# One sum of squares instead of two in the column products of further norm groups

## The chip, the cores and the metric

The kernel runs on one core of one Trainium2 chip. The metric is the device time of one execution in microseconds (us). It ran three times before the change: 1835.74, 1836.15 and 1836.15 us, with a median of 1836.15. Five engines work side by side and are named as in the profile: PE (matrix products; PEld is its loading of weights, which overlaps PE), DVE (vector engine), ACT (scalar engine), POOL (GpSimd) and SP (which here issues transfers). Engines wait for one another by semaphores.

## The reference

A small decoder trunk in f32 with two layers works on 528 tokens of width 1024 (16 meta tokens and 512 tokens). Each layer has a SwiGLU feed-forward at half weight, a token mixer, and a second feed-forward at half weight. The mixer is gated linear attention (GLA) in layer 0 and sliding-window attention (SWA) in layer 1. The SWA uses one set of keys and values made once, after layer 0. Every sub-layer is normed on its input and on its output:

```python
def rmsnorm(x, g):
    y = x * lax.rsqrt(jnp.mean(x * x, axis=-1, keepdims=True) + EPS)
    return y * g

for layer in range(2):
    g = norm_gains[layer]
    h = h + 0.5 * rmsnorm(swiglu(rmsnorm(h, g[0]), w_ffn_in[layer, 0], w_ffn_out[layer, 0]), g[1])
    hn = rmsnorm(h, g[2])
    mix = gla_mixer(hn, ...) if layer == 0 else swa_mixer(hn, ..., k_shared, v_shared)
    h = h + rmsnorm(mix, g[3])
    h = h + 0.5 * rmsnorm(swiglu(rmsnorm(h, g[4]), w_ffn_in[layer, 1], w_ffn_out[layer, 1]), g[5])
    if layer == 0:
        k_shared, v_shared = split(rmsnorm(h, g_kv) @ w_kv)
```

The change concerns the sum over the 1024 features in `mean(x * x)` and nothing else.

## The kernel before, in words

Features lie on the 128 partitions and tokens along the free axis. A row of 1024 features is therefore 8 tiles (`KD` = 8, index k), and `H` is the residual stream and `Y` the output of a sub-layer in that layout. Tokens are worked in two groups: `L0 = [(0, 272), (272, 256)]` in layer 0 and `L1 = [(16, 256), (272, 256)]` in layer 1. They are called group 0 and group 1 here (gi in the code).

**Exact products.** To keep f32 accuracy each operand is split into a high and a low half. The operand `x_<name>` of a projection is built by `Operand.build`: ACT scales H by the gain and rounds it (L591, the high half), and DVE makes the low half (L227 is the line through which all of DVE's operations are recorded). A projection then takes three matmuls for each weight tile and k: two with the high half, one with the low half. Weights are streamed from HBM (`raw`) and split in the same way by ACT (L295, L317) and DVE (`w`, `w_s`).

**A norm.** The squares of the 8 tiles are summed over k into a tile `acc_<name>` by `square_into` (L559 and L561 square on ACT, L562 adds on POOL). With `parts` 1 the first square starts the sum and each of the other seven goes to a scratch tile and is added by POOL. With `parts` 2 the last square (k = 7) is not added: ACT writes it straight into a second sum. Then `root` sums over the partitions: for each column chunk of 128 tokens (of 68, in the group of 272 tokens) and for each of the sums it issues one f32 matmul with a column of ones, into `st_<name>`. The profile shows each such f32 product as two matmuls. A chain of small operations follows (`av`, `yv`, `zv`, `wv`), on DVE for the post-norms and on POOL for most operands, which ends in a diagonal `dg_<name>`. A matmul with ones spreads it over the partitions as `r_<name>` (called the factor). For a post-norm (`Residual.run`) DVE multiplies Y by r, adds the product to H, and the next operand is built from that H, k by k, and its squares are summed. For an operand, r is copied to `R_<name>` (L619) and applied by DVE after the projection (`gu<-x,R`), so that the projection can begin before r is known.

**Order.** PE's order is written by hand: the program is a set of generators, driven by a planner (`Flow`) with a clock of its own. Each matmul advances the clock by what it charges: n/2400 us for n columns of the split type, at least 0.12 for an f32 product. When the clock passes the time for which a job is due, its next step is placed, and a job's `yield d` says after how much of the clock it goes on. Jobs are looked at (`flow.pump`) after each of the low-half matmuls of a projection. In `x_first` these come as the last four of every twelve matmuls (four weight tiles times three, for one k), and group 0 has 96 matmuls there (8 k) before group 1 begins with its own 96. The other engines' order is made by a scheduler from the program's dependences.

The delays that matter here:

- `Residual.run` waits `1.8 + (ADDED if parts == 1 else 0)` before the products of a post-norm (L645), then `DCHAIN` = 3.0 plus `factors[gi]` before its factor r (L528).
- `Operand.factors` waits `FACT` = 1.5, plus `ADDED` where `parts` is 1, before its products, then `CHAIN` = 5 or `DCHAIN`, and more by name, before r.
- `ADDED` = 1.4; `CROWDED` = 1.8 is the `factors[1]` of the post-norm named l1f1, `SLACK` = 1.0 that of l1m.

**Names.** `into(name, ...)` makes a pair: the residual step (post-norm) at the end of one sub-layer and the operand of the next. l0m stands between layer 0's first feed-forward and GLA, l0f1 between GLA and the second feed-forward, kv between that and the shared keys, l1m between layer 1's first feed-forward and SWA, and l1f1 between SWA and the last feed-forward. The profile leaves the last digit out, so l0f1 appears as l0f and l1f1 as l1f. The last post-norm, "out", is made without `into`.

Of the kernel before, what the change touches and what calls it, by code (L numbers as in the profile page):

```python
# [28 lines left out]
L0 = [(0, 272), (272, 256)]  # L29
L1 = [(16, 256), (272, 256)]  # L30
# [41 lines left out]
V_KVN = 96  # L72
# [72 lines left out]
def trunk_kernel(ctx: ExitStack, tc, a, out, last_out):  # L145
# [12 lines left out]
    vec = cp.tile([P, V_N], F32, name="vec")  # L158
# [8 lines left out]
    def pair_tile(name, dt=F32R):  # L167
        return hp.tile([P, 2, TOK], dt, tag="pair", name=name)
# [5 lines left out]
    def flat(t):  # L174
        return t.rearrange("p a t -> p (a t)")
# [25 lines left out]
    def gain(layer, i, k):  # L201
        c = V_GAIN + layer * 48 + i * 8 + k
        return vec[:, c : c + 1]
# [427 lines left out]
    class Residual:  # L631
# [44 lines left out]
        def turn(self, g, sums):  # L676
# [10 lines left out]
            def turn_four(into, src, c, q):  # L687
                b = into[c][q] = ps(f"turn_{self.name}{c}{q}")
                for k in range(4):
                    transpose(b[:, k * P : (k + 1) * P], src[:, 4 * q + k, o + c * P : o + (c + 1) * P])  # L690
# [460 lines left out]
    class Gated(Item):  # L1151
# [8 lines left out]
        def into(self, hid):  # L1160
            self.hid = hid
            scratch = flat(pair_tile(f"c{self.name}", F32))
            n = self.n
            self.u2, self.g1, self.v = (scratch[:, i * n : (i + 1) * n] for i in range(3))
            self.h = scratch[:, n : 3 * n]
# [706 lines left out]
    sp.dma_start(ident, a["ident"])  # L1872
    dve.memset(eps, 1e-6)

    def into(name, layer, i, half, gv, groups, parts=(1, 2), post=(1, 2)):
        nxt = Operand(name, gv, groups, parts=parts)
        return nxt, Residual(name, layer, i, half, nxt, post)


    nxt, fin = into("l0m", 0, 1, True, lambda k: gain(0, 2, k), L0, (1, 1))  # L1880
    ffn(x, L0, fin, True)
    x = nxt
    nxt, fin = into("l0f1", 0, 3, False, lambda k: gain(0, 4, k), L0)
    gla(x, fin)
    x = nxt
    nxt, fin = into("kv", 0, 5, True, lambda k: vec[:, V_KVN + k : V_KVN + k + 1], L0, (1, 1))
    nxt.more = BUSY
    fin.factors[0] = SLACK_KV
    ffn(x, L0, fin, tail=8)
# [2 lines left out]
    with tc.tile_pool(name="kp", bufs=1) as kp:  # L1892
        x, own = Operand("l1f0", lambda k: gain(1, 0, k), L1), nxt

        def again(gi):
            while (1, KD - 1) not in own.ready:
                yield SCORE
            for k in range(KD):
                x.build(gi, k)
                yield 1.0  # L1900

        kv, placed = shared_kv(nxt, kp, [again(0), again(1)])
        x.rt, x.rjob, x.roots = nxt.rt, nxt.rjob, 0
        nxt, fin = into("l1m", 1, 1, True, lambda k: gain(1, 2, k), L1, (1, 1))
        fin.factors[1] = SLACK
        roots = kp.tile([P, 2, 4], F32, name="roots")
        nxt.column = [(roots[:, 0, 2 * g : 2 * g + 2], roots[:, 1, 2 * g : 2 * g + 2]) for g in range(2)]
        ffn(x, L1W, fin)
        x = nxt
        nxt, fin = into("l1f1", 1, 3, False, lambda k: gain(1, 4, k), L1, post=(2, 2))  # L1910
        fin.factors[1] = CROWDED
        flow.wait(placed)
        swa(x, kv, fin)
# [96 lines left out]
```

## Time and profile before

| what | value |
| --- | --- |
| median of the three runs | 1836.15 us |
| the profiled execution's own time | 1835.98 us |
| its span, first instruction to last | 1834.2 us |
| granted clock of PE over the span | 9 of 10 or more in all 40 slices |
| adds of squares on POOL for post-norms (L562) | 77, of 0.74 us in the median |

A row of a group reads: line, engine, operation, output <- inputs with their shapes, count, busy time, mean length in ns, then the idle time of the engine before it and what ended it. A row of the timeline reads: start, length, engine, line, operation, output <- inputs, count of like instructions that were joined into the row, and in brackets the idle time before it with its releaser. Matmuls overlap, so the length of a joined row runs past the start of the next, and the time that PE gives to a group is read from start to start. A row of the waits reads: the waiting engine and line, what it waited for, then the total, the number of waits and the longest. Of a kernel's stretch the windows give the engine's busy time.

### The profile page before, as it was taken

How to read it: one execution, taken by the hardware profiler on the slowest of the kernel's cores; microseconds unless marked ns; L12 is line 12 of the kernel's file. 1: busy time of each engine (PE TensorE's matmuls, PEld its weight loads, DVE VectorE, ACT ScalarE, POOL GpSimd, SP SyncE). 2: the span in 40 equal slices, each digit the busy share in tenths (PEclk: the TensorE clock that was granted, in tenths of full speed). 3: DMA queues.
4: the chain of work that ended last, by engine and by line, in shares of the span. 5: the costliest groups of instructions: out<-in, count | busy, mean ns of one | idle time of the engine just before them, and what ended most of it. 6: DMA issues, size and time to landing. Idle time of an engine off the chain costs nothing.

```text
span 1834.2 us, 38756 instructions
## 1 busy us (share of the span) xinstructions
PE 1825.8 (100%) x14696; PEld 1772.8 (97%) x14696; DVE 1481.2 (81%) x3029; ACT 1137.5 (62%) x2643; POOL 333.3 (18%) x499
## 2 busy tenths in 40 slices
PE   9999999999999999999999999999999999999998
PEld 9999999999999999999999899999988898999998
DVE  6889888679785788888878789888776678899884
ACT  6666665655576566665665566666666866666564
POOL 2210101330001411010133110202320142111122
PEclk9999999999999999999999999999999999999999
DMA  7755758433234366666853565759430226667681
GB/s 246 197 153 152 173 147 235 170 117 88 57 129 144 106 174 156 155 168 151 249 188 104 137 166 140 185 150 242 168 107 22 70 93 165 161 153 177 152 255 51
DMA packets 146251, 277.45 MB, mean 151 GB/s; under 512 B 16400, under 2 KB 36752, under 8 KB 146064
## 3 DMA queue, kind: packets, MB, share of 16 engines
q1 hardware_dynamic: 114208, 198.15, 33.9%
q0 software_dynamic: 31424, 76.23, 20.8%
q8 instruction: 115, 1.88, 0.4%
q10 hardware_dynamic: 432, 0.59, 0.1%
q14 instruction: 72, 0.59, 0.1%
HBM read 236.05 MB, written 38.34 MB: 150 GB/s over the span
## 4 chain that ended last, share of the span: by engine, by line
PE 92%; DVE 3%; ACT 2%; DMA 1%; issue 1%; SPq 0%; DVEq 0%; ACTq 0%
PE a L206 30%; PE x L206 18%; PE y L206 17%; PE c L206 14%; PE d L206 7%; ACT s L1729 1%; PE o L206 1%; PE po L206 1%; DVE w L227 1%; DMA raw<-in_w_in 1%; DMA H<-in_h 1%; DVE s L227 1%; DVE w_s L227 1%; DVE raw L227 1%; PE ps L206 0%
## 5 line engine op out<-in xcount | busy, mean ns | idle before, releaser
L227 DVE TENSOR_TENSOR w<-raw,w 128x512 fp32r<-128x512 f32 (+1 forms) x556 | 356.7, 666 | 28.8 <-ACT w L295 23.7
L227 DVE TENSOR_TENSOR w_s<-raw,w_s 128x512 fp32r<-128x512 f32 (+1 forms) x432 | 275.2, 647 | 78.3 <-ACT w_s L317 74.2
L317 ACT ACTIVATE w_s<-raw 128x512 fp32r<-128x512 f32 (+1 forms) x432 | 250.9, 593 | 94.4 <-DVE raw L227 90.8
L227 DVE TENSOR_TENSOR raw<-raw,raw 128x512 f32<-128x512 f32 (+1 forms) x312 | 194.9, 631 | 3.2
L376 POOL DMA_DIRECT2D raw<-in_w_in x112 | 105.6, 988 | 449.3 <-DVE w L227 169.0
L317 ACT ACTIVATE w<-raw 128x512 fp32r<-128x512 f32 (+1 forms) x324 | 185.0, 590 | 0.0
L295 ACT ACTIVATE w<-raw 128x512 fp32r<-128x512 f32 x232 | 133.8, 620 | 2.1 <-PE y L206 1.2
L206 PE MATMUL y<-hidl0f,w 128*128 128x272 f32 (+1 forms) x960 | 119.4, 285 | 0.0
L206 PEld LDWEIGHTS y<-hidl0f,w 128*128 128x128 f32 x960 | 118.0, 188 | 0.2
L206 PE MATMUL a<-zl0f_t,w_s 128*128 128x264 f32 x864 | 117.3, 285 | 0.0
L206 PE MATMUL y<-hidl1f,w 128*128 128x256 f32 (+1 forms) x768 | 114.9, 310 | 0.0
L206 PE MATMUL a<-zl1f_t,w_s 128*128 128x256 f32 x864 | 114.0, 281 | 0.0
L206 PEld LDWEIGHTS y<-hidl1f,w 128*128 128x128 f32 x768 | 105.0, 188 | 8.5
L1274 POOL DMA_DIRECT2D kept_y<-dn x32 | 36.8, 1149 | 405.6 <-DVE w_s L227 164.4
L206 PEld LDWEIGHTS a<-zl0f_t,w_s 128*128 128x128 f32 x864 | 110.3, 188 | 0.0
L562 POOL TENSOR_TENSOR acc_post<-acc_post,sq_post 128x256 f32<-128x256 f32 (+1 forms) x77 | 61.2, 796 | 264.4 <-ACT sq_post L561 260.9
L206 PEld LDWEIGHTS a<-zl1f_t,w_s 128*128 128x128 f32 x864 | 107.2, 188 | 0.0
L206 PE MATMUL x<-x_l0m,w 128*128 128x256 f32 (+1 forms) x768 | 102.2, 289 | 0.0
L206 PE MATMUL x<-x_l0f,w 128*128 128x256 f32 (+1 forms) x768 | 98.3, 287 | 1.6 <-ACT w L295 0.8
L206 PEld LDWEIGHTS x<-x_l0f,w 128*128 128x128 f32 x768 | 94.9, 189 | 3.0 <-DVE w L227 1.4
L206 PEld LDWEIGHTS x<-x_l0m,w 128*128 128x128 f32 x768 | 95.8, 188 | 1.6 <-issue 0.8
L206 PE MATMUL x<-x_l1f,w 128*128 128x256 f32 (+1 forms) x576 | 93.2, 321 | 0.0
(551 smaller groups left out, 4116.1 us busy)
## 6 DMA issues: line engine op xcount, KB each, us to landing
raw<-in_w_in SPq DMA_DIRECT2D x408, 256.0 KB, 4.3
raw<-in_w_in POOLq DMA_DIRECT2D x112, 256.0 KB, 5.4
raw<-in_w_down SPq DMA_DIRECT2D x128, 192.0 KB, 2.4
raw<-in_gla_in SPq DMA_DIRECT2D x52, 256.0 KB, 3.3
raw<-in_w_last SPq DMA_DIRECT2D x48, 256.0 KB, 5.2
kept_y<-dn POOLq DMA_DIRECT2D x16, 528.0 KB, 8.3
raw<-in_w_out SPq DMA_DIRECT2D x32, 256.0 KB, 3.4
kept_y<-dn POOLq DMA_DIRECT2D x16, 512.0 KB, 8.8
```

The lines of the kernel that those rows point to most:

```text
L206: inst = pe.matmul(o, lhs, rhs, start=start, stop=stop, skip_group_check=onto)
L227: made = op(*args, **named)
L295: high = act.activation(w[:, 0, :m], raw[:, :m], AF.Copy)
L317: act.activation(w[:, 0, :m], src, AF.Copy)
L376: added = pool.dma_start(r, src, accum_op=ALU.add)
L562: pool.tensor_tensor(sums[0][:, :n], sums[0][:, :n], t[:, :n], op=ALU.add)
L1274: pool.dma_start(y_sum[:, 2 * self.q : 2 * self.q + 2, o : o + 2 * n], self.y[:, :, : 2 * n], accum_op=ALU.add)
L1729: act.activation(s[:, c], s[:, c], AF.Exp, scale=rc[:, c % 2 : c % 2 + 1], bias=nm[:, c : c + 1], accum_out=den[:, c : c + 1],)
```

## The change

The defaults of `into` become one sum for both groups, in the operand (`parts`) and in the post-norm (`post`). The explicit `(1, 1)` of l0m and kv, which set the operand, become superfluous and are dropped; that of l1m stays. The explicit `post=(2, 2)` of l1f1 is dropped, so that it takes the default.

```diff
-    def into(name, layer, i, half, gv, groups, parts=(1, 2), post=(1, 2)):
+    def into(name, layer, i, half, gv, groups, parts=(1, 1), post=(1, 1)):
         nxt = Operand(name, gv, groups, parts=parts)
         return nxt, Residual(name, layer, i, half, nxt, post)
...
-    nxt, fin = into("l0m", 0, 1, True, lambda k: gain(0, 2, k), L0, (1, 1))
+    nxt, fin = into("l0m", 0, 1, True, lambda k: gain(0, 2, k), L0)
...
-    nxt, fin = into("kv", 0, 5, True, lambda k: vec[:, V_KVN + k : V_KVN + k + 1], L0, (1, 1))
+    nxt, fin = into("kv", 0, 5, True, lambda k: vec[:, V_KVN + k : V_KVN + k + 1], L0)
...
-        nxt, fin = into("l1f1", 1, 3, False, lambda k: gain(1, 4, k), L1, post=(2, 2))
+        nxt, fin = into("l1f1", 1, 3, False, lambda k: gain(1, 4, k), L1)
```

What each name has, as number of sums of (group 0, group 1):

| name | operand before | operand after | post-norm before | post-norm after |
| --- | --- | --- | --- | --- |
| l0m | (1, 1) | (1, 1) | (1, 2) | (1, 1) |
| l0f1 | (1, 2) | (1, 1) | (1, 2) | (1, 1) |
| kv | (1, 1) | (1, 1) | (1, 2) | (1, 1) |
| l1m | (1, 1) | (1, 1) | (1, 2) | (1, 1) |
| l1f1 | (1, 2) | (1, 1) | (2, 2) | (1, 1) |

The number changes in eight groups, six of post-norms and two of operands. The delays that depend on it (`ADDED`) change with it. The opening operand, with (2, 2), and "out", with (1, 2), are not touched.

## The prediction

> **What bounds the kernel now.** I read the page's first part and chain, then the waits of the matmul engine, then the timeline around the column products.
>
> ```profile
> span 1834.2 us, 38756 instructions
> PE 1825.8 (100%) x14696; PEld 1772.8 (97%) x14696; DVE 1481.2 (81%) x3029; ACT 1137.5 (62%) x2643; POOL 333.3 (18%) x499
> PE 92%; DVE 3%; ACT 2%; DMA 1%; issue 1%; SPq 0%; DVEq 0%; ACTq 0%
> ```
> ```profile
> PE busy L1821 <- DVE eps L227: 1.0, 1, 1.0
> PE x L206 <- ACT w L295: 0.8, 2, 0.4
> PE x L206 <- DVE w L227: 0.7, 2, 0.3
> ```
>
> PE is the kernel: 1825.8 of 1834.2 us busy, 92% of the chain, and the whole list of what it waited for (these are its largest entries) holds about 3 us. So the time is the sum of PE's instructions. Removing some saves their time one for one; any wait that is newly exposed on PE costs one for one. I therefore count two things: matmul pairs that go, and lost cover ahead of the instructions that PE reads next.
>
> **What goes.** A group of 256 tokens has two column chunks. The timeline of PE shows both kinds of group for the same norm (start, duration, operation, count):
>
> ```profile
> 1311.84 0.50 PE L206 MATMUL st_post_l1m<-ones,acc_post 128*128 128x1 f32 x4
> 1312.20 3.82 PE L206 MATMUL y<-hidl1f,w 128*128 128x256 f32 x30
> 1329.38 0.95 PE L206 MATMUL st_post_l1m<-ones,acc_post 128*128 128x1 f32 x8
> 1330.18 1.65 PE L206 MATMUL x<-x_l1m,w 128*128 128x256 f32 x12
> ```
>
> With one sum the products hold PE from 1311.84 to 1312.20, 0.36 us for 4 matmuls; with two from 1329.38 to 1330.18, 0.80 us for 8. The difference is 0.44 us a group. By the diff's arguments eight groups change: the second group of the post-norms l0m, l0f1, kv and l1m, both groups of post-norm l1f1, and the second group of operands l0f1 and l1f1. 8 x 0.44 = **-3.5 us**. It is all on PE, so all on the path.
>
> **What is added.** Eight adds on GpSimd, one per group:
>
> ```profile
> L562 POOL TENSOR_TENSOR acc_post<-acc_post,sq_post 128x256 f32<-128x256 f32 x56 | 42.7, 763 | 190.1 <-ACT sq_post L561 186.8 <-DVE H L227 3.2
> 366.78 0.40 ACT L559 ACTIVATE acc_post<-Y 128x256 f32<-128x256 f32 x1
> 369.39 0.95 PE L206 MATMUL st_post_l0m<-ones,acc_post 128*128 128x1 f32 x8
> ```
>
> That is 8 x 0.76 = 6.1 us on an engine that is 18% busy. In l0m the last square, which today goes straight into its own sum, ends at 367.18; the products start at 369.39. The add would end near 368.0 even in today's order, so PE would not wait for it. Two adds of the next norm stand on GpSimd's queue about there; they cost at most another 1.8 us, and the products themselves come later (next part). I cost the adds at nothing; without that cover one add is 0.76 us on the path.
>
> **What moves.** This is where the gain may go. A group with one sum waits ADDED = 1.4 more on the planner's clock before its products are put into PE's order (L645, L605). The clock charges 0.107 to a 256-token matmul and jobs are placed only at the last four of every twelve, so 1.4 becomes 12 matmuls. What those take in fact, and what follows from it at the tightest place, the second group of post-norm l1f1, is in these rows:
>
> ```profile
> 1484.17 0.95 PE L206 MATMUL st_post_l1f<-ones,acc_post 128*128 128x1 f32 x8
> 1484.97 4.46 PE L206 MATMUL x<-x_l1f,w 128*128 128x256 f32 x36
> 1489.28 0.50 PE L206 MATMUL st_l1f<-ones,acc_l1f 128*128 128x1 f32 x4
> 1487.74 0.42 DVE L227 TENSOR_TENSOR dg_post_l1f<-ident,yv_post_l1f 128x256 f32<-128x256 f32 x1
> L206 PE MATMUL x<-x_l1f,w x81: 274/280/365, 1480.3 to 1491.0; 128*128 128x256 f32 x81
> 1491.14 0.60 PE L206 MATMUL r_post_l1f<-dg_post_l1f,ones 128*128 128x256 f32 x2
> 1491.78 0.43 DVE L227 TENSOR_TENSOR r_post_l1f<-Y,r_post_l1f 128x256 f32<-128x256 f32 x1 [3.61 <-PE r_post_l1f L206]
> 1492.24 0.42 DVE L227 TENSOR_TENSOR H<-r_post_l1f,H 128x256 f32<-128x256 f32 x1
> 1492.70 0.51 ACT L591 ACTIVATE x_l1f<-H,vec 128x256 fp32r<-128x256 f32 x1 [2.62 <-DVE H L227]
> ```
>
> From 1484.97 to 1489.28 there are 36 matmuls in 4.31 us, 0.12 us each: 12 are **1.44 us**. The factor's product r_post starts after 81 of the 96 first-group matmuls; 15 are left, about 1.8 us and 0.25 for r_post itself. From r_post to the first build of the second group (multiply, add, scale) it is 1491.14 to 1493.21, 2.07 us. The two are equal: no slack today. The diagonal is ready at 1488.16, 3 us ahead, so the place of r_post is set by the planner, not by data. Twelve matmuls later only 3 are left, and PE has nothing else in its order: it stands about **+1.4 us**. The later builds shift with the first one, and PE with them, so this is paid once.
>
> The same shift of 1.44 us strikes the other second groups against the slack of their last build:
>
> ```profile
> 379.05 13.52 PE L206 MATMUL x<-x_l0m,w 128*128 128x272 f32 x111
> 388.61 0.96 DVE L227 SCALAR_TENSOR_TENSOR x_l0m<-H,vec,x_l0m 128x256 fp32r<-128x256 f32 x1
> 392.41 0.50 PE L206 MATMUL st_l0m<-ones,acc_l0m 128*128 128x1 f32 x4
> 617.93 7.82 PE L206 MATMUL x<-x_l0f,w 128*128 128x256 f32 x63
> 623.55 0.48 DVE L227 SCALAR_TENSOR_TENSOR x_l0f<-H,vec,x_l0f 128x256 fp32r<-128x256 f32 x1
> 625.58 0.95 PE L206 MATMUL st_l0f<-ones,acc_l0f 128*128 128x1 f32 x8
> ```
>
> - l0m: the 111 matmuls are 3 of the first group, 96 of the second and 12 of the next unit. The last build's low half is first read 16 matmuls before 392.41, at 390.5; it is ready at 389.57. Slack 0.9 us against 1.44: **+0.5 us**; bounds 0 (the scheduler may put the build ahead of a weight split) and 1.4.
> - l0f1: the low half is first read 4 matmuls before 625.58, at 625.1, and ready at 624.03. Slack 1.1: **+0.4 us**, bounds 0 and 1.4.
> - l1m: its r_post moves to where l1f1 has it today, where PE shows no wait: **+0.1 us**, bounds 0 and 1.4 (if its scale comes late).
> - kv has the sizes and places of l0m; its builds are not held behind weight splits at that point. I take 0 and let l0m's 0.5 bound it.
> - l1f1's first group: its products are among the attention's last output products and its builds are read some 5 us on; 0.
>
> **The operands.** For l1f1 and l0f1 the second operand factor is moved as well. Rows of l1f1, the last one from a window of 0.04 us around the first product that reads the last tile of h:
>
> ```profile
> 1507.91 0.95 PE L206 MATMUL st_l1f<-ones,acc_l1f 128*128 128x1 f32 x8
> 1515.75 0.59 PE L206 MATMUL r_l1f<-dg_l1f,ones 128*128 128x256 f32 x2
> 1516.38 0.38 ACT L619 ACTIVATE R_l1f<-r_l1f 128x256 f32<-128x256 f32 x1 [5.32 <-PE r_l1f L206]
> 1516.80 0.42 DVE L227 TENSOR_TENSOR gu<-x,R_l1f 128x256 f32<-128x256 f32 x1 [5.27 <-ACT R_l1f L619]
> 1516.80:1534.10 17.30, 17.20 (x32) 1.00 0.38 91
> 1533.37 0.69 DVE L227 TENSOR_TENSOR hidl1f<-gu,hidl1f 128x512 fp32r<-128x512 f32 x1
> 1534.89 0.63 PE L206 MATMUL y<-hidl1f,w 128*128 128x512 f32 x2
> ```
>
> DVE sits idle 5.27 us for R, then is busy 17.20 of 17.30 us, up to the last tile of h, ready at 1534.06. PE reads it with the second matmul of that row, near 1535.1: slack 1.05 us. Nothing in between gives time back. The shift of R is 1.4 to 2.8 us (one or two places of the planner, here with matmuls twice as wide); taken at 2.25, PE stands **+1.2 us**, bounds 0 and 1.8. For l0f1, with 272-token tiles and fewer products in between, I take **+0.2 us**, bounds 0 and 1.0.
>
> **Sum.** -3.5 + 1.4 + 0.5 + 0.4 + 0.1 + 1.2 + 0.2 = **+0.3 us**. The profiled execution took 1835.98 us, its span and 1.8 around it; the median shown is 1836.15, 0.17 above. From the median the change gives **1836.4 us**.
>
> One more thing the adds can do is hold DVE (start, duration):
>
> ```profile
> 1812.23 0.16 DVE L227 TENSOR_TENSOR zv_post_out<-zv_post_out,av_post_out 128x2 f32<-128x2 f32 x1
> 1812.32 0.73 POOL L562 TENSOR_TENSOR acc_post<-acc_post,sq_post 128x256 f32<-128x256 f32 x1 [3.44 <-ACT sq_post L561]
> 1812.43 0.64 DVE L227 SCALAR_TENSOR_TENSOR wv_post_out<-zv_post_out 128x2 f32<-128x2 f32 x1
> ```
>
> A DVE operation of 0.16 us takes 0.64 here, and ends as the add of GpSimd beside it ends. So an added add may cost DVE up to 0.5 us by this row, 8 x 0.5 = 4 us in all if each meets such an operation. DVE has 353 us idle and none of the eight adds falls into the stretch 1516.8 to 1534.1, where it has none, so I take 0; the upper bound for the place where it matters (l1f1's last builds) is one such meeting, 0.5 us.
>
> The Trainium skill, page "SBUF — State Buffer", section "Who interferes with whom", states the reason as a rule: a DVE instruction with two SBUF inputs and a GpSimd instruction that reads SBUF exclude each other, the later one being blocked for the whole of the earlier. The two rows agree with it, though the blocked operation has tiny inputs. By the rule all eight adds speak against the change; the sum would be +0.8 instead of +0.3 if one meets the path.
>
> **Rivals.**
> 1. *Everything but l1f1's first build is covered.* For it: a shift of 1.44 us against slacks of 0.9 to 1.1 leaves only small remainders, and the tile scheduler may order DVE anew. Then -3.5 + 1.4 = -2.1, **1834.1 us**; if the planner leaves r_post where it is too, -3.5, 1832.6.
> 2. *Slower: the late R of l1f1 backs up DVE.* DVE has no gap from 1516.8 on, so lateness there also holds weight splits, and with them the transfers that refill their buffers, and the next tiles PE needs. It decides from the point where all stalls pass 3.5 + 3.7 = 7.2 us, against the 3.8 of my sum; R's shift at its end of 2.8, paid twice (tile of h, then weights), and 1.4 in l0m and l0f1 each give 1.4 + 2.8 + 2.8 + 2.8 = 9.8, so -3.5 + 9.8 = +6.3, **1842.4 us**. Against it: PE shows 0.7 us of waits for DVE's splits in the whole kernel.
> 3. *The products do not cost their time.* If PE's next weights had to be waited for anyway, the 0.44 us would not come back. Against it: the matmul after the one-sum products starts as promptly as after the two-sum ones. Then 0 + 3.8 = +3.8, **1839.9 us**.
>
> **How the numbers follow.** 0.2% (3.7 us) is about what a measurement of this kernel can tell from no change. The sum as it stands, and mixtures near it: 0.50. Rival 1: 0.23, of which 0.05 beyond -0.2%. Rival 2: 0.19. Rival 3: 0.08, half of it over the bound. So faster 0.05, slower 0.23, same 0.72. The range runs from 1833.2 (rival 1 with most of the saving) to 1840.6 (rival 3 and the near part of rival 2); it leaves out about 2 in 10, mostly above.
>
> **What would show it.** PE should have 32 matmuls fewer; the eight groups' products 4 instead of 8, 0.36 us. In x_l1f's timeline r_post should stand after 93 of the 96, and PE should wait some 1.4 us for ACT's x_l1f: the largest new entry in the list of waits. Waits for DVE's x_l0m, x_l0f and for hidl1f should be 0.2 to 1.8 us each. Wrong would make it: r_post still at 81; a wait of PE over 2 us at any one place; a stall on acc_post's add; or a planner that, with 0.24 us less charged per group, places other jobs elsewhere.

## The result and the profile after

The changed kernel takes 1843.66 us in the median of six executions (1841.39 to 1846.8), against 1836.17 before (1835.74 to 1836.27). The ratio is 1.0043 with a 95% interval of 1.0032 to 1.0054: slower by 7.5 us, outside the predicted range. The executions lie far apart for this kernel, and they order by the granted clock of PE: 1841.39 and 1842.51 us at 1.000, 1843.59 at 0.999, 1843.73 and 1845.44 at 0.998, 1846.8 at 0.997. The profiled one took 1843.59.

The page's first lines and the largest waits of PE, after (waiting engine and line, what it waited for, total, times, longest):

```profile
span 1841.8 us, 38721 instructions
PE 1825.1 (99%) x14664; PEld 1769.1 (96%) x14664; DVE 1482.4 (80%) x3029; ACT 1140.3 (62%) x2643; POOL 342.6 (19%) x507
```
```profile
PE x L206 <- DVE w L227: 2.3, 3, 1.6
PE o L206 <- ACT pm L1755: 1.6, 2, 1.2
PE r_kv L206 <- POOL dg_kv L520: 1.4, 1, 1.4
PE x L206 <- ACT w L295: 1.3, 2, 1.0
PE sa L206 <- DMA q<-turn: 1.0, 1, 1.0
PE x L206 <- ACT x_l1f L591: 0.7, 1, 0.7
PE x L206 <- ACT x_l0m L591: 0.6, 1, 0.6
PE x L206 <- ACT x_l0f L591: 0.5, 1, 0.5
```

The parts that the diff names are there: 14664 matmuls instead of 14696, 32 fewer, and 507 instructions on POOL instead of 499. But PE's busy time fell by 0.7 us only, and six of these eight entries were not there before (the waits for w from DVE and ACT were, with 0.7 and 0.8 us; the opening's wait for eps, 1.0 us in both, is left out here). To see where it lost time, I compared the start of the same matmul in both traces at the edges of the stages. "Lost" is the difference gained in the stage plus 0.44 us for each changed group in it.

| stage, up to | changed kernel behind by | in the stage | groups | lost |
| --- | --- | --- | --- | --- |
| first product of l0m | 0.03 | | | |
| l0m and GLA, to the first product of l0f1 | 1.30 | 1.27 | 1 | 1.7 |
| l0f1 and its feed-forward, to kv | 1.79 | 0.49 | 2 | 1.4 |
| kv and the next feed-forward, to l1m | 2.61 | 0.82 | 1 | 1.3 |
| l1m and the attention, to l1f1 | 3.87 | 1.26 | 2 | 2.1 |
| products of l1f1 | 7.69 | 3.82 | 2 | 4.7 |

So in this trace 3.5 us were saved and 11.2 lost. The largest loss stands in l1f1. The timeline of PE there (start, duration, operation, count, idle time before and its releaser), and windows of the same stretch (PE's busy time and count, then the granted clock, the DMA share and GB/s):

```profile
1495.57 0.59 PE L206 MATMUL r_post_l1f<-dg_post_l1f,ones 128*128 128x256 f32 x2
1497.68 7.00 PE L206 MATMUL x<-x_l1f,w 128*128 128x256 f32 x57 [0.71 <-ACT x_l1f L591]
1511.83 7.15 PE L206 MATMUL x<-x_l1f,w 128*128 128x512 f32 x23 [1.58 <-DVE w L227]
```
```profile
1512.00:1513.00 1.00, 1.00 (x5) 1.00 0.92 297
1513.00:1516.50 3.50, 3.50 (x11) 0.51 0.84 271
1516.50:1518.50 2.00, 2.00 (x10) 1.00 0.34 104
```

r_post stands after 93 of the 96 matmuls, as predicted, and PE waits for the first build; start to start that costs 0.87 us. What was not predicted: a wait for w (1.84 us start to start), and right after it 3.4 us in which the clock is granted at half and 512-token matmuls start every 0.43 us instead of 0.23. Eight such matmuls are 1.6 us more.

### The profile page after: what moved, and what is told of

It is laid out like the page before. It is cut to its first block, busy times and chain, and to the rows that moved or that the text cites. A ratio compares the mean times of both kernels' runs of the same rounds, so it can differ in the third digit from the quotient of the medians.

```text
span 1841.8 us, 38721 instructions
## 1 busy us (share of the span) xinstructions
PE 1825.1 (99%) x14664; PEld 1769.1 (96%) x14664; DVE 1482.4 (80%) x3029; ACT 1140.3 (62%) x2643; POOL 342.6 (19%) x507
## 4 chain that ended last, share of the span: by engine, by line
PE 91%; DVE 4%; ACT 2%; DMA 1%; issue 1%; POOL 1%; SPq 0%; DVEq 0%; ACTq 0%; POOLq 0%
PE a L206 30%; PE y L206 18%; PE x L206 15%; PE c L206 15%; PE d L206 8%; PE o L206 1%; DVE w L227 1%; ACT s L1729 1%; DMA H<-in_h 1%; PE po L206 1%; PE pt L237 0%; DMA raw<-in_w_in 0%; DVE raw L227 0%; PE sa L206 0%; DMA q<-turn 0%
## 5 line engine op out<-in xcount | busy, mean ns | idle before, releaser
L562 POOL TENSOR_TENSOR acc_post<-acc_post,sq_post 128x256 f32<-128x256 f32 (+1 forms) x83 | 66.2, 797 | 266.1 <-ACT sq_post L561 261.2
```

What stands on the lines that cost most here:

```text
L562: pool.tensor_tensor(sums[0][:, :n], sums[0][:, :n], t[:, :n], op=ALU.add)
```

## The experiments

**One sum without the added delay, and the delay without the sum.** The first kernel is the changed one, but the eight groups do not get ADDED; the second is the kernel before with ADDED in the eight groups.

```diff
+    NEW_POST = {("l0m", 1), ("l0f1", 1), ("kv", 1), ("l1m", 1), ("l1f1", 0), ("l1f1", 1)}
+    NEW_OPERAND = {("l0f1", 1), ("l1f1", 1)}
...
-    yield 1.8 + (ADDED if self.parts[gi] == 1 else 0) + self.sums[gi]
+    yield 1.8 + (ADDED if self.parts[gi] == 1 and (self.name, gi) not in NEW_POST else 0) + self.sums[gi]
...
+    (the second kernel: "or (self.name, gi) in NEW_POST" in place of "and ... not in")
```

> The eight groups have one sum and GpSimd's eight adds, but keep the places that the planner gave them before: the 1.4 of ADDED is left out for these eight groups alone. Theory A (the added wait on the planner's clock is what costs; the adds are hidden): the whole saving comes out, 1836.2 - 3.5 = about 1832.6 us, PE has 32 matmuls fewer and none of the new waits for x_l0m, x_l0f, x_l1f and for w behind them. Theory B (the adds themselves cost, by making PE wait for the sums or by holding DVE): the time stays where the change put it, 1840 us or more, and PE's waits name acc_post or the stalls of the changed kernel stand unmoved.

> The opposite half: the kernel before with two sums everywhere it had them, no added work at all, but the 1.4 of ADDED in the eight groups. Theory A: the whole loss without the saving, 1836.2 + 7.5 + 3.5 = about 1847 us. Theory B: no loss, 1836 us within 1.

One sum without the delay: 1834.95 us against 1835.94, ratio 0.9994 (0.9985 to 1.0003), runs within 1.3 us. The delay alone: 1844.75 us, ratio 1.0048 (1.0031 to 1.0065), with a granted clock of 1.000 in all four executions. That is a loss of 8.8 us; less the saving of 3.5 it leaves 5.3, and the changed kernel's fastest execution, at 1.000 too, lies 5.2 above the kernel before. So the delay carries the loss, and no loss by the adds shows in the changed kernel; what its other executions took beyond that goes with the clock. But without the delay the saving comes out at 1.0 instead of 3.5, and these new entries in PE's waits say why:

```profile
PE st_post_l1f L208 <- POOL acc_post L564: 0.4, 1, 0.4
PE r_l0f L208 <- POOL dg_l0f L522: 0.3, 1, 0.3
PE st_post_kv L208 <- POOL acc_post L564: 0.2, 1, 0.2
```

The products now come before the add has ended, or the diagonal behind them is late. Start to start PE loses 0.25 to 0.58 us at five places, 2.0 us of the 2.5 that are missing; in l0m, where the prediction had read the add's cover, it loses nothing. The delay is what hides the other adds; it is too long for what hangs on it.

**The change without l1f1, and l1f1 alone.**

```diff
# first kernel, from the changed one
-        nxt, fin = into("l1f1", 1, 3, False, lambda k: gain(1, 4, k), L1)
+        nxt, fin = into("l1f1", 1, 3, False, lambda k: gain(1, 4, k), L1, (1, 2), (2, 2))
# second kernel, from the one before
-        nxt, fin = into("l1f1", 1, 3, False, lambda k: gain(1, 4, k), L1, post=(2, 2))
+        nxt, fin = into("l1f1", 1, 3, False, lambda k: gain(1, 4, k), L1, (1, 1), (1, 1))
```

> The change everywhere but in l1f1, which keeps (2, 2) for its post-norm and (1, 2) for its operand. In the changed kernel's trace PE is 3.9 us behind the kernel before when the attention's output products end, and 7.7 us at the end. If the parts add up, this kernel takes about 1840.2 us (+4); if l1f1 alone carries the loss, about 1834 (four or five groups' saving and small stalls). The runs should lie close together, because the half-clock stretch of the changed kernel stands in l1f1.

> The kernel before with the change in l1f1 alone (three groups). If the parts add up: about 1836.2 + 3.8 = 1840 us, with PE waiting some 0.9 us for x_l1f and some 1.6 us for w in the next units, followed by about 3.4 us at half clock in some executions; so the runs should spread by 2 to 5 us as those of the changed kernel do. If the loss needs the lateness gathered earlier, it is under 1837.

Without l1f1: 1841.46 us (1839.75 to 1843.69), ratio 1.0031 (1.002 to 1.0042). l1f1 alone: 1836.17 us, ratio 1.0002 (0.9993 to 1.0011). The parts do not add up: the first lies above the 1840.2 expected of it, and l1f1 alone costs nothing, without the spread (nine of ten executions within 1.1 us, one at 1838.28). l1f1 alone pays its wait for the first build, 1.32 us start to start, and gets 1.3 back from three groups; the wait for w is not there. And the kernel without l1f1 spreads too: its half-clock stretch stands in the attention, after PE waited for the transfers of q:

```profile
1362.63 1.23 PE L206 MATMUL sa<-kz,q 64*128 64x144 f32 x8 [1.83 <-DMA q<-turn]
1364.00:1366.00 2.00, 2.00 (x7) 0.50 0.10 25
```

So what looks like a loss of l1f1 begins earlier. Before it lies l1m.

**The change without l1m, l1m alone, and l1m with its factor in place.** What hangs on l1m's last build is read in the code: the evacuation of its products and the turn that rotates q wait until the build (1, 7) is placed, and so do the splits of the next weights (a loop in the program asks for that build). In PE's timeline the first turn and the first scores (sa), before and after:

```profile
1349.92 0.64 PE L206 MATMUL turn<-q,sel 128*32 128x256 f32 x8
1356.88 0.76 PE L206 MATMUL sa<-kz,q 64*128 64x144 f32 x8
```
```profile
1353.73 0.64 PE L206 MATMUL turn<-q,sel 128*32 128x256 f32 x8
1361.67 0.82 PE L206 MATMUL sa<-kz,q 64*128 64x144 f32 x8 [1.01 <-DMA q<-turn]
```

PE reached l1m 2.6 us late, but the turn is 3.8 and the scores are 4.8 late.

```diff
# without l1m, from the changed kernel
-        nxt, fin = into("l1m", 1, 1, True, lambda k: gain(1, 2, k), L1, (1, 1))
+        nxt, fin = into("l1m", 1, 1, True, lambda k: gain(1, 2, k), L1, (1, 1), (1, 2))
# l1m alone, from the kernel before
+        nxt, fin = into("l1m", 1, 1, True, lambda k: gain(1, 2, k), L1, (1, 1), (1, 1))
# l1m alone with its factor in place: the same, and
-        fin.factors[1] = SLACK
+        fin.factors[1] = SLACK - ADDED
```

> The change everywhere but in l1m, whose second post-norm group keeps two sums. Theory C: l1m's group, placed later, moves the start of the attention (its evacuations and its turn wait for the last build of that group), makes the first scores wait for the transfers of q, pushes the first group of l1f1 some 8 us back and so brings up the wait for w in l1f1 and the half clock behind it. Then without it: about 3.1 us late on reaching l1m, nothing more in the attention, and 0.5 in l1f1 as where l1f1 was changed alone: 1839 us, runs close together (within 1 us), no wait of PE for q, the first r_post of l1f1 near 1475 and not 1480. Rival: l1f1's waits come from l1f1's own groups, and the attention's from the lateness gathered before: 1842 us or more, with the same spread as the changed kernel.

> The kernel before with one sum in the second group of post-norm l1m and nothing else. Theory C: -0.4 for the products, +1.3 to +3.2 in the attention (the amounts of the changed kernel and of the one with all but l1f1): 1837 to 1839 us with a spread of some us, PE waiting 1 to 2 us for q, the first r_post of l1f1 some 8 us later. Rival (the shift is covered as predicted, +0.1 - 0.4): 1835.7.

> As the kernel with l1m alone changed (1838.5 us), with the delay before l1m's factor shortened by the same 1.4: the products stand 12 matmuls later, the factor and the builds behind it where they stood before. Theory C (it is the place of the factor, through the last build, that upsets the attention): the loss goes, the saving stays, 1835.6 us, runs within 1 us, turn and first scores where they were. Rival (the sum or the add upsets it): 1837 to 1840 with the same spread.

Without l1m: 1838.94 us (1838.57 to 1839.9), ratio 1.0016 (1.0007 to 1.0026); no wait for q, no half clock, the first r_post of l1f1 at 1476.2, and in l1f1 only the 1.33 us for the first build (and waits under 0.5 us each). l1m alone: 1838.46 us (1836.76 to 1842.43), ratio 1.0013 (1.0003 to 1.0023). The waits in its attention are for the probabilities (pm), 1.7 us in all, more than for q (0.2), and the first r_post of l1f1 is 4.3 us later and not 8, so the expected place was only half right; a half-clock stretch follows them:

```profile
PE o L206 <- ACT pm L1755: 1.7, 2, 1.2
1394.20:1398.00 3.80, 3.80 (x27) 0.56 0.24 52
```

With the factor in place: 1835.83 us (1835.01 to 1836.02), ratio 0.9998 (0.9988 to 1.0007); no wait over 0.4 us behind the opening, no spread. One sum, the add and the later products are all still there. What upsets the attention is the place of the factor; that it does so through the last build is read from the program and was not tested by itself. l1m costs 1843.66 - 1838.94 = 4.7 us of the whole. Set beside the kernel without l1m, the changed kernel loses 1.7 of it in the attention and 3.1 in l1f1.

**The order of the splits in l1f1.** Weight splits that wait for the last build ask for it every 0.5 of the planner's clock, each unit by itself. A unit is two raw tiles. In the changed kernel's order on DVE, the unit that PE reads first (raw196 below) is split third, behind two others; in the kernel before it is first, and in the changed kernel without l1m second. These are the raw tiles that DVE splits behind l1f1's last build, in the programs' order:

```
before:       raw196_0 raw196_512 raw197_0 raw197_512 raw198_0 raw198_512 raw199_0 raw199_512
without l1m:  raw197_0 raw197_512 raw196_0 raw196_512 raw198_0 raw198_512 raw199_0 raw199_512
after:        raw198_0 raw198_512 raw197_0 raw197_512 raw196_0 raw196_512 raw199_0 raw199_512
```

The unit is also second where l1m alone, l1f1 alone, or all but l1f1 is changed; it is third with the delay alone. So the turned order takes the shifts of l1m and of l1f1 together. DVE's splits in the changed kernel's trace fit it: the fifth tile ends at 1511.78, and PE goes on at 1511.83.

```profile
1507.65 2.86 DVE L227 TENSOR_TENSOR w<-raw,w 128x512 fp32r<-128x512 f32 x4
1511.10 0.68 DVE L227 TENSOR_TENSOR w<-raw,w 128x512 fp32r<-128x512 f32 x1
```

The experiment lets the units that wait for l1f1's last build go one after the other and changes nothing else:

```diff
+            held = any(x.name == "l1f1" for x in building)
             while any((1, KD - 1) not in x.ready for x in building):
                 yield 0.5
+            if held and not split_jobs[i - 1].done:
+                yield split_jobs[i - 1]
```

> The changed kernel, with the weight splits that wait for l1f1's last build let go one unit after the other in the order in which PE uses them. In the changed kernel's order on DVE the unit that PE needs first is split third, as fifth and sixth tile. Theory E (this turned order makes the wait of 1.8 us for w and, through it, the half clock in l1f1): the wait for w there is under 0.3 us, no half clock near 1513, and the median falls by 1.8 and by the 1.7 of the half clock, to about 1840 us; the spread that stays comes from the attention. Rival (the last build is too late for any order): the wait stays over 1 us and the time at 1842 us or more.

1839.61 us (1838.59 to 1844.02), ratio 1.0023 (1.0014 to 1.0032): 4.1 us less than the changed kernel. PE's row in l1f1 runs through:

```profile
1504.51 10.52 PE L206 MATMUL x<-x_l1f,w 128*128 128x256 f32 x63
```

The wait of 1.84 us was the turned order. The half clock that stood right behind it is gone from this trace too, and the median fell by more than the wait alone. Four of the eleven executions still took over 1840.4 us, three of them at a clock of 0.998; where those lost it no trace of this kernel shows. In the traces of the kernels with l1m alone (above) and with CROWDED 0.4 (below) it was in the attention.

**kv alone, and with its chain on DVE.** In the changed kernel one small operation of GpSimd takes 4.91 us. Beside it DVE runs eight subtractions for weight splits without a gap (first two rows: after; last two: before):

```profile
989.46 4.91 POOL L485 TENSOR_TENSOR zv_kv<-yv_kv 128x2 f32<-128x2 f32 x1
989.42 4.89 DVE L227 TENSOR_TENSOR w<-raw,w 128x512 fp32r<-128x512 f32 x8
```
```profile
986.52 0.19 POOL L485 TENSOR_TENSOR zv_kv<-yv_kv 128x2 f32<-128x2 f32 x1
986.86 4.89 DVE L227 TENSOR_TENSOR w<-raw,w 128x512 fp32r<-128x512 f32 x8
```

Both end at 994.3 to 994.4. Before, the same operation had ended when DVE's run began, and most of the next ones took 0.5 us each beside it, in turns with DVE. The diagonal dg_kv now ends at 997.73, and PE stands 1.4 us for it. The experiments change post-norm kv alone, then move the second chain of operand kv to DVE:

```diff
# both, from the kernel before: into("kv", ..., L0, (1, 1), (1, 1))
# the second also, in Operand.factors:
+            same = CHAIN + self.more
+            if self.name == "kv" and gi == 1:
+                eng = dve
             later = rstd(self.accs[gi], n, D, False, f"{self.name}_{o}", eng, ...)
             delay = next(later)
+            if self.name == "kv":
+                delay = same
```

> The kernel before with one sum in the second group of post-norm kv alone. In the changed kernel GpSimd's zv_kv of the operand kv takes 4.9 us, as long as the eight subtractions for w that run on DVE beside it, and PE waits 1.4 us for dg_kv. Theory D (the shift moves that step into the run of subtractions): the same here, zv_kv near 4.9 us, PE's wait near 1.4, +1.0 in all: 1836.9 us. Rival (it needs the lateness gathered before kv, by chance of phase): zv_kv under 1 us, no wait, 1835.5.

> The same, with the small chain of the operand kv's second group on DVE in place of GpSimd, placed on PE's order as before. Theory D (GpSimd is held by DVE's run of two-input operations): no wait of PE for dg_kv, the saving alone, about 1835.5 us. Rival (r_kv is late for another reason, its products or its place): the wait stays at 1 us or more, 1836.5 or above.

kv alone: 1837.1 us (1836.77 to 1837.65) against 1836.04, with zv_kv at 4.92 us and this wait:

```profile
PE r_kv L206 <- POOL dg_kv L520: 1.5, 1, 1.5
```

With the chain on DVE: 1835.03 us (1834.7 to 1835.56), and no such wait. The two runs do not overlap, though each one's interval against the kernel before holds 1 (1.0006, 0.9995 to 1.0016; 0.9994, 0.9984 to 1.0004). Theory D fits both: the same products and sums, and 2.1 us between the engines on which a chain of 128 x 2 numbers is worked.

**The changed kernel with CROWDED 0.4.** One number is changed (`CROWDED = 0.4`), which puts r_post of l1f1 back.

> The changed kernel with CROWDED 0.4 in place of 1.8, so that only the factor of the second post-norm group of l1f1 goes back by the 1.4 that its products were moved. If l1f1's place of r_post makes its share of the loss, PE's wait for x_l1f (0.9 us by its spacing) goes and the wait for w behind the last build (1.8) shrinks by some 0.6, with the half clock rarer: about 1840.5 to 1842 us against 1843.7. The waits in l0m, l0f1, kv and the attention stay. If that place does not matter, 1843.7 with the same waits.

1842.6 us in the median of four (1840.83 to 1847.12), ratio 1.0039 (1.0025 to 1.0053). The wait for x_l1f is gone; the wait for w is not smaller (1.77 us start to start, the same turned order of the splits). With that spread the time does not tell the two expectations apart. The profiled execution was the slowest, 1847.12, and shows two half-clock stretches, the first in the attention, with no wait longer than 0.5 us in the nine before it:

```profile
1400.00:1405.00 5.00, 4.25 (x35) 1.00 0.08 17
1405.50:1411.50 6.00, 6.00 (x37) 0.50 0.00 0
1514.60:1517.40 2.80, 2.80 (x7) 0.50 0.83 282
```

**A wait of known length.** The kernel before with one number changed (`CROWDED = 4.0`), so that PE waits for the first build of l1f1's second group and nothing else is touched.

> The kernel before with CROWDED 4.0 in place of 1.8 and all sums as they were: only r_post of l1f1's second group is placed later, behind the last of the 96 matmuls, and PE waits for the first build. A wait of 1.8 us is expected (15 matmuls of 0.12). If a wait of that length can start a stretch at half clock (as after 1.8 and 1.9 us in two of the runs, not after 1.3 and 1.5), some executions take about 1838 us and some 1.7 more, at a granted clock of 0.998 to 0.999; if the clock is not touched by such a wait, all lie at 1838 within 0.5.

1837.94 us (1837.53 to 1838.55), ratio 1.0011 (1.0002 to 1.002): the wait of 1.87 us start to start is paid one for one, and none of ten executions lost clock. The 15 matmuls of cover that the prediction counted were thus counted right. What starts a half-clock stretch is not the length of one wait alone.

**The saving without the shifts.** Seven groups with one sum: l0m and l0f1 without the delay, l1m and l1f1 with the factor put back, kv's chain on DVE; operand l0f1 keeps two sums.

```diff
-    CROWDED = 1.8
+    CROWDED = 0.4
+    NEW_POST = {("l0m", 1), ("l0f1", 1)}        # these two without ADDED
...
+    into("l0m", ..., L0, (1, 1), (1, 1)); into("l0f1", ..., L0, (1, 2), (1, 1))
+    into("kv", ..., L0, (1, 1), (1, 1)); into("l1m", ..., L1, (1, 1), (1, 1)); into("l1f1", ..., L1, (1, 1), (1, 1))
-        fin.factors[1] = SLACK
+        fin.factors[1] = SLACK - ADDED
```

> Seven of the eight groups with one sum, each with the added delay taken back where the runs showed that it can be: l0m and l0f1 post without it, l1m and l1f1 with a shorter delay before the factor (-0.4 and 0.4), kv with its operand's second chain on DVE; operand l0f1 keeps two sums. By the parts: 7 x 0.44 = 3.1 us less, and up to 0.4 more from kv: 1832.7 us, no new wait of PE over 0.5 us. If moving several places upsets the order elsewhere, 1835 or more.

1832.35 us in the median of eleven (1831.92 to 1832.85) against 1835.93 (1835.43 to 1836.69), ratio 0.998 (0.9972 to 0.9989): 3.6 us faster than the kernel before and 11.3 faster than the changed one, with no wait of PE over 0.5 us behind the opening. The largest entries:

```profile
PE busy L1827 <- DVE eps L228: 1.0, 1, 1.0
PE x L207 <- DVE w L228: 1.0, 3, 0.3
PE x L207 <- ACT w L296: 0.9, 2, 0.5
```

## Why the prediction was wrong

**The saving (-3.5) was right.** 0.44 us a group comes out where nothing else moves: seven groups gave 3.6 us in the last kernel, with up to 0.4 of it from kv's chain on DVE.

**The adds (0) were right for the changed kernel**, where the delay covers them; without it PE waits 0.2 to 0.6 us in places. Of the two covers named, the later products are the one that counts; the other was read in l0m alone, where it holds.

**r_post in l1f1 (+1.4) was right**: 1.32 and 1.33 us where l1f1 met an undisturbed attention, 0.87 in the changed kernel.

**l0m (+0.5) and l0f1 (+0.4) were too small**: 1.05 us (0.30 and 0.75) and 1.37 (0.30, 0.42 and 0.65), by spacing. The mechanism was right. The error was to carry the shift of 1.4 us unchanged to the last build. DVE's rows for the residual of k = 6 and the two splits beside it, before and after:

```profile
383.45 0.41 DVE L227 TENSOR_TENSOR H<-r_post_l0m,H 128x256 f32<-128x256 f32 x1
383.79 1.50 DVE L227 TENSOR_TENSOR w<-raw,w 128x512 fp32r<-128x512 f32 x2
```
```profile
383.71 1.50 DVE L227 TENSOR_TENSOR w<-raw,w 128x512 fp32r<-128x512 f32 x2
386.94 0.41 DVE L227 TENSOR_TENSOR H<-r_post_l0m,H 128x256 f32<-128x256 f32 x1
```

Before, this addition had its turn just ahead of the splits; now it comes behind them, and is 3.5 us late instead of 1. DVE's order is fixed in the program, so a small delay cost a whole place, with the splits between. I also read the slack from the low half alone, while it is ACT's high half that PE now waits for.

**kv (0) was wrong by 1.4 us.** I bounded it by l0m and looked at its builds; they are in time. The step that failed is "I take 0", with l0m as its bound: the chain of the operand behind them was not looked at, and the shift set it beside DVE's run. I had weighed GpSimd against DVE only in the other direction, an add that holds DVE for 0.5 us. Here DVE held GpSimd for ten times that. The Trainium skill, page "SBUF — State Buffer", section "Who interferes with whom", gives the rule that bears on it: two SBUF inputs on DVE and a reading GpSimd instruction exclude each other. The trace agrees that the two engines held each other up; that GpSimd was shut out over eight DVE instructions (4.91 us) and not one is what these runs add.

**l1m (+0.1) is where the prediction failed most.** Its builds were indeed in time for PE: no wait for x_l1m appears. The term priced only PE's own use of them. What else waits for the last build was not listed: the evacuation, the turn and with it the first scores, and the splits of weights, which in this kernel are tied to the last build by a wait in the program. The attention lost 2.1 us by the table, and with l1f1's own shift the order of l1f1's splits was turned (1.84 us), which was followed by half clock (1.6). Without l1m's group 4.7 of the 7.5 us are gone. Shown are the group (4.7 us), the place of its factor (the loss goes when it is put back) and the turned order (4.1 us); that the polls of the planner's clock turned it is read from the program.

**Operand l1f1 (+1.2) did not happen.** With l1f1 alone, its second R comes 2.27 us later, as forecast, and yet the last tile of h is ready at 1534.11 instead of 1534.06. The step that failed is "Nothing in between gives time back": the scheduler ordered DVE anew, so that two of the five splits between R and that tile went ahead of R and three other operations behind the tile. For operand l0f1 (+0.2) no wait is seen either.

**Rival 2 had the sign and not the place.** It let the late R back up DVE's splits in l1f1. PE did wait for splits there, but those behind the last build, before R mattered, and in a turned order. Its argument against itself, that PE shows only 0.7 us of waits for splits in the whole kernel, says only that a balanced order had been found, not how it behaves once shifted. Its 1842.4 us lies near the measured time by luck: the 1.4 in l0m and l0f1 each is about what they cost, but the 5.6 for R did not occur, and l1m, kv and the half clock stood in its place. Of its signs of being wrong, the prediction had named a planner that places other jobs elsewhere; it gave it no term. Rivals 1 and 3 did not occur.

**The half clock was in none of the terms.** It cost 1.6 us in the profiled execution and accounts for most of the 5 us between the fastest and the slowest: a mean clock lower by 0.003 (1.000 and 0.997) over 1845 us is some 5.5 us of missing clock.

## What to carry to other kernels

When a step moves in an order written by hand, list everything that waits for its result, not only the engine that is the bound: evacuations, gates on loads and splits, polls. Price a shift on an engine whose order is fixed by the place that it falls back to, not by the shift. A longer delay that covers new work should be taken back behind that work, where the chain has room; here this, with one small chain moved to DVE and one operand left as it was, turned a loss of 7.5 us into a gain of 3.6.

## What the runs showed of the hardware

A GpSimd operation on 128 x 2 numbers took 4.91 us beside eight gapless two-input operations of DVE (4.89 us together), whose run had begun 0.04 us before it. It did so again in the runs that brought the two to the same phase (4.92 with kv alone, 4.75 with the splits in order). In the kernel before it ended ahead of DVE's run and took 0.19; most of the next ones then took some 0.5 us each beside that run.

PE's granted clock fell to half for 3.41 us, at a cost near 1.7, after gaps of 2.07 us (1511.83, changed kernel), 2.23 us (1362.6, without l1f1) and 2.00 us (1514.4, CROWDED 0.4) between two starts. It also fell in the attention's small matmuls, 2.2 us after a gap of 1.50 us (l1m alone), and for 6.83 us with no wait above 0.5 us just before (CROWDED 0.4). A gap of 1.90 us in dense matmuls did not bring it in ten executions.

So the length of a gap does not decide, and the traces show what else may. In each of the fifteen, every change of the granted clock lies a whole number of steps of 3.413 us behind the first one: 442 and 443 steps in the changed kernel, 410, 412, 442 and 443 with CROWDED 0.4. Where a gap falls in these steps therefore matters. An estimate: counted as columns at the planner's charge of 2400 per us, PE's matmuls filled 0.36, 0.38, 0.38, 0.40 and 0.19 of the step just before each of the five drops. The step that holds the gap of 1.90 us was filled to 0.41 and kept the full clock. Between the opening and the f32 products that end each kernel, the emptiest steps that kept it were filled to 0.40, in front of the late dg_kv, so the two kinds meet there. No run here set the phase, so what decides stays an estimate.

The Trainium skill, page "TensorE: Matmul & The Clock Gate", section "What's actually happening", says that the clock goes to half after an idle window of about 3.4 us and back after a busy one of that length, and that the windows run freely, so that the transition depends on where in the window the work lands. The half speed and the length of the steps agree with these traces; the windows before the drops were partly filled, not idle.
